# A chunked RWKV-7 block: the state's decay moves from TensorE and ScalarE to GpSimd and VectorE, and the output products get a stream of their own

## The chip, the cores and the metric

The kernel runs on one core of a Trainium2 chip, in one launch. A core has five engines that work at the same time, each through its own queue in order: PE (TensorE, matrix products into PSUM), ACT (ScalarE), DVE (VectorE), POOL (GpSimd, which also issues DMAs) and SP (which only issues DMAs). The metric is device time in microseconds (us) of one execution. Three runs of the kernel before gave 1114.17 to 1115.25, median 1114.42 us.

## The reference

It is one block of a network for a sequence of 512 tokens of width 1024: an RWKV-7 time mix with 16 heads of width 64, a depthwise convolution of 31 taps beside it, a gated merge of the two, and a feed-forward of width 2816. What matters here is the recurrence of the time mix. Each head has a 64 x 64 state that decays and takes a rank-one update at every token:

```python
def step(S, inp):
    r_t, w_t, k_t, v_t, a_t, b_t = inp
    sa = jnp.einsum('bhvk,bhk->bhv', S, a_t)
    S = S * w_t[:, :, None, :] + sa[..., None] * b_t[:, :, None, :] + v_t[..., None] * k_t[:, :, None, :]
    y = jnp.einsum('bhvk,bhk->bhv', S, r_t)
    return S, y
```

Its `y` is normalized per head, gets a bonus and a gate, and is multiplied by `w_rwkv_out`; the convolution's result is normalized over all channels and multiplied by `w_conv_out`.

## The kernel before

All arrays lie with channels on the 128 partitions and the 512 tokens along the free axis, so there are 8 channel tiles (`ct` 0 to 7), of two heads each. Large products are done in three matmuls on a value and its rounding rest (`acc3`: high by high, high by low, low by high); one such output tile is 24 matmuls of 128x512, called `dn` in the profile. Weights come in halves of 256 KB: on POOL's queue by two DMAs (`wh`, and `wl`, which adds the weights onto a copy that ACT has negated) or, when `sc.fast` is off, on SP's queue by one DMA (`wf`) and a subtraction on DVE.

The recurrence is done in 8 chunks of 64 tokens per channel tile. For each channel tile `prep` builds the decayed keys, `solve` inverts the triangular systems of all chunks, `values` lays out the values, and `chain(ct)` goes through the 8 chunks one after the other. One step of the chain is: a product of the state `SV` with the keys (`zt<-SV,AR`), a copy by ACT (`zs`), a product with the inverse (`zt<-zs,Pbd`), two copies by ACT (`UV`), and the update of the state. For the update PE adds the old state itself, as a product with the identity matrix (`zt<-SV,cs` in the profile, since the identity lies in the tile `cs`), and the product `zt<-UV,bkT` on top of it in PSUM; two ACT instructions of 64x64, one for each head, multiply the sum by the decay of the chunk `dL` and write the next `SV`. The first chunk has no old state, the last makes no next one, so there are 6 identity products in a chain and 48 in all, and 7 pairs of ACT instructions in a chain. The output products `yp` are issued in the chain itself, in two halves, after the fourth chunk and after the last.

The order of the instructions around this is set by a planner (`Sched`). Each stream records its instructions; the planner has a cost for every kind of instruction, keeps a clock for each engine, and takes from the heads of all streams the one that can start first, within 0.15 us the one of the most urgent priority: chain 0, `prep` and `values` 2, `solve` and `finish` 3, large products 4, the 31 taps of the convolution (`taps`, on DVE) 5. What comes out is a fixed order on each engine; on the chip an engine waits at the head of its queue, whatever stands behind. Streams wait for events, which are posted when all that was recorded ahead of them has been issued: `chain(ct)` waits for `("chain", ct - 1)`, `("val", ct)` and `("solve", ct)`; `solve(ct)` waits for `("chain", ct - 1)` before it writes the inverse tile `Pbd`, of which there is one.

The taps are 31 passes of DVE over a 128x512 tile for each channel tile (`cacc` and `cpad` are their two running sums, `ca` holds their input and their result). When all 8 are done, `conv_norm` normalizes and writes `CH` and `CL`, which the products of `w_conv_out` read. Behind the chains come the products of the gates and of `w_rwkv_out`, then those of `w_conv_out`, `w_out` and the feed-forward, all of them `dn` matmuls.

Of the kernel before, what the change touches and what calls it, by code (L numbers as in the profile page):

```python
# [9 lines left out]
F32 = mybir.dt.float32  # L10
F32R = mybir.dt.float32r
I32 = mybir.dt.int32
AF = mybir.ActivationFunctionType
ALU = mybir.AluOpType
# [3 lines left out]
P = 128  # L18
# [4 lines left out]
L = 64  # L23
NCH = T // L
# [6 lines left out]
WK = 4  # L31
WB = 6
WT = 4
LB = {"mu_r": 2, "mu_k": 2, "mu_v": 1}
NWO = 3
BUFS = (2, 2, 2, 2, 2, 1, 1)
# [45 lines left out]
def tile_hybrid_block(ctx, tc, xT, cst, prm, dwp, wl1, w2g, w_in, w_ro, w_co, w_o,  # L82
# [277 lines left out]
    sc = Sched()  # L360
# [18 lines left out]
    V, G, S = Engine("DVE", nc.vector), Engine("POOL", nc.gpsimd), Engine("ACT", nc.scalar)  # L379
    PE, SY = Engine("PE", nc.tensor), Engine("SP", nc.sync)  # L380

    def pool(stack, name, bufs, **k):
        return Pool(stack.enter_context(tc.tile_pool(name=name, bufs=bufs, **k)), bufs)

    cp = pool(ctx, "cp", 1)
    wp = pool(ctx, "wp", WT)
    turn = itertools.count()
    tp = pool(ctx, "tp", 1)
    sp = pool(ctx, "sp", 2)
# [3 lines left out]
    py = pool(ctx, "py", 1, space=PSUM)  # L393

    def tmp(name, tag=None, bufs=1, cols=T):
        return tp.tile([P, cols], F32, tag=tag or name, bufs=bufs, name=name)
# [9 lines left out]
    ident = cs[:, C_ID:C_ID + P]  # L406
# [10 lines left out]
    def vec(name, ct, lo=0, hi=P):  # L417
        j = VECS.index(name) * NT + ct
        return pr[lo:hi, j:j + 1]
# [7 lines left out]
    def der(d, ct):  # L427
        return drv[:, d * NT + ct:d * NT + ct + 1]

    E, O = slice(0, 64), slice(64, 128)  # L430
# [40 lines left out]
    def colstat(dst, src, rhs, blocks=4):  # L471
        for b in range(blocks):
            PE.matmul(dst(b), lhsT=src[:, b * P:(b + 1) * P], rhs=rhs, start=True, stop=True)

    def bcast(ps, lhs, blocks=4):
        for b in range(blocks):
            PE.transpose(ps[:, b * P:(b + 1) * P], lhs(b), ident)

    def spread(r8, rx):
        S.activation(out=rx.rearrange("p (a v) -> p a v", v=HD),  # L480
                     in_=r8.unsqueeze(2).to_broadcast([P, 8, HD]), func=AF.Copy)


    def rsqrt(v, n):
        y, t, w = (sp.tile([P, n], F32, tag=g_, bufs=2, name=g_) for g_ in ("ry", "rt", "rw"))
        V.tensor_scalar(out=y.bitcast(I32), in0=v.bitcast(I32), scalar1=-0.5, scalar2=RSQ,
                        op0=ALU.mult, op1=ALU.add)
        for _ in range(3):
            V.tensor_mul(t, v, y)
            V.scalar_tensor_tensor(out=w, in0=t, scalar=-0.5, in1=y, op0=ALU.mult, op1=ALU.mult)  # L490
            V.scalar_tensor_tensor(out=y, in0=w, scalar=1.5, in1=y, op0=ALU.add, op1=ALU.mult)
        return y
# [72 lines left out]
    for k in range(NT):  # L565
        if k == WK:
# [4 lines left out]
                               op0=ALU.mult, op1=ALU.subtract)  # L571
# [11 lines left out]
    def normed():  # L583
        for k in range(NT):
# [7 lines left out]
                    op0=ALU.mult, op1=ALU.add)  # L592
# [3 lines left out]
                    op0=ALU.mult, op1=ALU.add)  # L596
# [7 lines left out]
    def act(n_):  # L604
        if n_ not in acts:
            acts[n_] = hp.tile([P, NT, T], F32, tag=n_, name=n_)
        return acts[n_]
# [73 lines left out]
    def ktmp(name, bufs=1, cols=T):  # L681
        pool = kp if name in ("mu_v", "ep") else kq
        return pool.tile([P, cols], F32, tag=name, bufs=bufs, name=name)

    def lerp(ps, dmu, nm, ct):
        t_ = ktmp(nm, bufs=LB[nm])
        S.activation(out=t_, in_=ps, func=AF.Identity, scale=der(dmu, ct))
        V.scalar_tensor_tensor(out=t_[:, 1:T], in0=ps[:, 0:T - 1], scalar=vec(nm, ct),
                               in1=t_[:, 1:T], op0=ALU.mult, op1=ALU.add)
        return t_  # L690
# [41 lines left out]
    def low_out(ct, c0, n, nm):  # L732
        wf_, wh_, wl_ = (wp.tile([P, n], d_, tag=nm + x_, bufs=1, name=nm + x_)
                         for x_, d_ in (("f", F32), ("h", F32R), ("l", F32R)))
        SY.dma_start(out=wf_, in_=w2g[ct][:, c0:c0 + n])
        split(wf_, wh_, wl_)
        return wh_, wl_

    def lerp_of(key, dmu, nm, ct):
        def then(ps):  # L740
            st[ct][key] = lerp(ps, dmu, nm, ct)
        return then

    def once(fn):
        fn()
        yield from ()
# [209 lines left out]
    def chain(ct):  # L956
        s_ = st[ct]
        if ct:
            yield ("chain", ct - 1)
        yield ("val", ct)  # L960
        yield ("solve", ct)
        AR, GR, UV, SV, pb, bkT, dL = (s_[n] for n in ("AR", "GR", "UV", "SV", "pb", "bkT", "dL"))
        yp = None

        def outputs(cs_):
            for c in cs_:
                if c > 0:
                    for par, R in ((0, E), (1, O)):
                        PE.matmul(yp[R, c, :], lhsT=SV[R, c, par, :], rhs=AR[R, c, 2, :],
                                  start=c == 1, stop=False, skip_group_check=True)  # L970
            for c in cs_:
                for par, R in ((0, E), (1, O)):
                    PE.matmul(yp[R, c, :], lhsT=UV[:, c, par, :], rhs=GR[:, c, par, :],
                              start=False, stop=True, skip_group_check=True)

        for c in range(NCH):
            zt = pc.tile([P, 7, L], F32, tag="ch", name="zt")
            PE.matmul(zt[:, 0:2, :], lhsT=AR[:, c, 0:2, :], rhs=SV[:, c, :, :],
                      start=True, stop=True)
            zs = sp.tile([P, 2, L], F32, tag="zs", name="zs")  # L980
            S.activation(out=zs, in_=zt[:, 0:2, :], func=AF.Copy)
            PE.matmul(zt[:, 5:7, :], lhsT=pb[:, c, :], rhs=zs, start=True, stop=True)
            for par, R in ((0, E), (1, O)):
                S.activation(out=UV[R, c, par, :], in_=zt[R, 5 + par, :], func=AF.Copy)
            if c < NCH - 1:

                if c > 0:
                    PE.matmul(zt[:, 3:5, :], lhsT=ident, rhs=SV[:, c, :, :],
                              start=True, stop=False)
                PE.matmul(zt[:, 3:5, :], lhsT=bkT[:, c, :], rhs=UV[:, c, :, :],  # L990
                          start=c == 0, stop=True)
                for par, R in ((0, E), (1, O)):
                    S.activation(out=SV[R, c + 1, par, :], in_=zt[R, 3 + par, :], func=AF.Identity,
                                 scale=dL[R, c:c + 1])
            if c == NCH // 2 - 1:
                yp = s_["yp"] = py.tile([P, NCH, L], F32, tag="y", name="yp")
                outputs(range(0, NCH // 2))
        outputs(range(NCH // 2, NCH))
        sc.post(("chain", ct))
        sc.spawn(once(lambda: finish(ct)), 3)  # L1000

    def finish(ct):
        s_ = st[ct]
        g2 = low_out(ct, 2 * P, P, "g2")
        yp = s_["yp"].rearrange("p c t -> p (c t)")
        sq = tmp("sqy", "sq", 2)
        S.activation(out=sq, in_=yp, func=AF.Square)
        ys = tmp("ys")
        S.activation(out=ys, in_=yp, func=AF.Identity, scale=vec("gn_w", ct))
        ss = pm.tile([P, 4, WS], F32, tag="fi", bufs=1, name="ssy")  # L1010
        colstat(lambda b: ss[:, b, :], sq, sel2v)
        n0 = sp.tile([P, 8], F32, tag="n1", bufs=1, name="n1")
        V.tensor_scalar_add(n0.rearrange("p (a b) -> p a b", b=2), ss[:, :, 0:2], GN_EPS)
        r = rsqrt(n0, 8)
        rx = tmp("rxy", "sq", 2)
        spread(r, rx)
        bc = pm.tile([P, T], F32, tag="fi", bufs=1, name="bcy")
        bcast(bc, lambda b: rx[:, b * P:(b + 1) * P])
        V.tensor_mul(ys, ys, bc)
        V.scalar_tensor_tensor(out=ys, in0=ys, scalar=vec("gn_b", ct), in1=act("ya")[:, ct, :],  # L1020
                               op0=ALU.add, op1=ALU.add)
        gp = pm.tile([P, T], F32, tag="fi", bufs=1, name="gp")
        acc3(gp, *g2, [0], lambda k: GH, lambda k: GL, True, True)
        V.tensor_mul(act("ya")[:, ct, :], ys, gp)
        s_.clear()
        sc.post(("ya", ct))


# [94 lines left out]
    for ct in range(1, NT):  # L1123
        dense_tile(w_in[NT + ct], lerp_of("tk", D_OMK, "mu_k", ct), need=(("keys", ct - LB["mu_k"]),) if ct >= LB["mu_k"] else (),
                   ev=("k", ct))
# [5 lines left out]
    for ct in range(NT):  # L1131
        for g_, pri in ((prep, 2), (values, 2), (chain, 0), (taps, 5)):
            sc.spawn(g_(ct), pri)
# [19 lines left out]
    mid = {}  # L1153
# [222 lines left out]
    for h in range(2):  # L1376
        c = HALF[h]
# [83 lines left out]
```

## Time and profile before

| | |
|---|---|
| median of 3 runs | 1114.42 us |
| the profiled execution's own time | 1110.63 us |
| its span, first to last instruction | 1108.9 us |
| granted TensorE clock, mean | 0.986 |
| busy: PE, DVE, ACT, POOL | 1061.3, 731.5, 568.2, 103.8 us |

The profile is one execution. Its busy times are unions of the instructions' records; matmuls are pipelined, so their records overlap and a busy PE is not a PE at its peak. A row of a timeline has the start in us from the span's start, the time, the engine, the line, the operation, output<-inputs, the shape and the count; in brackets stands how long the engine had been idle and what ended it. Everything that the planner orders bears the number of the one line that issues it, so groups are told apart by the names of their tiles.

### The profile page before, as it was taken

Reading aid. Unit: us, or ns where it says so; the run is one execution under the profiler, and the core shown is the slowest. Engines: PE = TensorE matmul, PEld = TensorE weight load, DVE = VectorE, ACT = ScalarE, POOL = GpSimd, SP = SyncE. Lnnn points to the kernel's source line nnn. Section 1 sums busy time; section 2 is a strip of 40 time slices with the busy share of each in tenths; the row PEclk is TensorE's granted clock in tenths of the full one; section 3 lists DMA queues with packets and bytes.
Section 4 is the critical chain, followed back from the end, with each engine's and each line's share of the span. In section 5 each row is a group of like instructions: output and inputs, shape, how many; then the busy total and the mean of one; then the engine's idle time right before and its main releaser. Section 6 shows DMA issues by size and latency. Waiting matters only on the chain.

```text
span 1108.9 us, 18596 instructions
## 1 busy us (share of the span) xinstructions
PE 1061.3 (96%) x7066; PEld 860.2 (78%) x7066; DVE 731.5 (66%) x1511; ACT 568.2 (51%) x1197; POOL 103.8 (9%) x172
## 2 busy tenths in 40 slices
PE   7799999999899999989999999999999999999996
PEld 5577787877787777768788888998888888888885
DVE  5878899899898999998553366365444444433324
ACT  5556666777777777555572235344333333323321
POOL 0003322211313222010000000000000000000000
PEclk9899999999899999999999999999999999999998
DMA  6115745434546454144232236102223222333312
GB/s 240 46 40 119 145 98 122 82 70 95 104 98 122 102 114 101 33 86 152 77 105 96 87 104 204 62 1 81 93 94 95 95 95 95 91 100 115 105 48 76
DMA packets 68872, 107.74 MB, mean 97 GB/s; under 512 B 15152, under 2 KB 20656, under 8 KB 68784
## 3 DMA queue, kind: packets, MB, share of 16 engines
q1 hardware_dynamic: 48912, 70.38, 20.2%
q0 software_dynamic: 19872, 36.18, 16.2%
q8 instruction: 56, 0.92, 0.3%
q14 instruction: 32, 0.26, 0.1%
HBM read 102.34 MB, written 2.10 MB: 94 GB/s over the span
## 4 chain that ended last, share of the span: by engine, by line
PE 83%; DVE 6%; ACT 4%; issue 1%; DMA 0%; DVEq 0%; ACTq 0%
PE dn L225 34%; PE dn L300 29%; PE zt L300 5%; PE psf L225 2%; PE wo L225 2%; PE yp L300 2%; PE gps L300 1%; ACT Mt L300 1%; PE lora L300 1%; DVE AR L300 1%; DVE GR L300 1%; DVE cacc L300 1%; DVE cpad L300 1%; PE ssy L300 1%; PE psn L225 1%
## 5 line engine op out<-in xcount | busy, mean ns | idle before, releaser
L225 ACT ACTIVATE wh<-wf 128x512 fp32r<-128x512 f32 x140 | 86.7, 619 | 219.2 <-PE dn L225 209.3
L225 DVE TENSOR_TENSOR wl<-wf,wh 128x512 fp32r<-128x512 f32 x140 | 94.4, 675 | 125.2 <-ACT wh L225 125.0
L300 PE MATMUL dn<-HH,wh 128*128 128x512 f32 x408 | 168.8, 414 | 0.0
L300 PE MATMUL dn<-HH,wl 128*128 128x512 f32 x408 | 168.1, 412 | 0.0
L300 PE MATMUL dn<-HL,wh 128*128 128x512 f32 x408 | 167.4, 410 | 0.0
L225 PE MATMUL dn<-FHL,wh 128*128 128x512 f32 x320 | 127.7, 399 | 0.0
L225 PE MATMUL dn<-FHH,wh 128*128 128x512 f32 x320 | 126.2, 394 | 0.0
L225 PE MATMUL dn<-FHH,wl 128*128 128x512 f32 x320 | 125.4, 392 | 0.0
L225 PE MATMUL dn<-FH,wh 128*128 128x512 f32 (+1 forms) x332 | 101.3, 388 | 0.0
L300 PEld LDWEIGHTS dn<-HH,wl 128*128 128x128 f32 x408 | 78.0, 191 | 14.4 <-issue 0.5
L300 PEld LDWEIGHTS dn<-HH,wh 128*128 128x128 f32 x408 | 77.8, 191 | 14.6 <-issue 0.7
L300 PEld LDWEIGHTS dn<-HL,wh 128*128 128x128 f32 x408 | 77.7, 190 | 14.6 <-issue 0.5
L300 ACT ACTIVATE wh<-wf 128x512 fp32r<-128x512 f32 x69 | 42.9, 627 | 78.5 <-PE dn L300 71.2
L300 DVE SCALAR_TENSOR_TENSOR cacc<-ca,dw,cacc 128x512 f32<-128x512 f32 x105 | 78.1, 744 | 0.0
L300 POOL DMA_DIRECT2D wl<-in_w_in_dram x69 | 60.4, 886 | 180.8 <-ACT wl L300 149.0
L300 DVE SCALAR_TENSOR_TENSOR cpad<-ca,dw,cpad 128x512 f32<-128x512 f32 x98 | 73.0, 745 | 0.1
L300 DVE TENSOR_TENSOR wl<-wf,wh 128x512 fp32r<-128x512 f32 x69 | 47.3, 688 | 38.6 <-ACT wh L300 38.6
L225 PEld LDWEIGHTS dn<-FH,wh 128*128 128x128 f32 x332 | 61.5, 188 | 13.9
L225 PEld LDWEIGHTS dn<-FHH,wh 128*128 128x128 f32 x320 | 60.1, 188 | 15.7
L225 PEld LDWEIGHTS dn<-FHH,wl 128*128 128x128 f32 x320 | 60.1, 188 | 14.3
L225 PEld LDWEIGHTS dn<-FHL,wh 128*128 128x128 f32 x320 | 60.1, 188 | 13.6
L225 PE MATMUL dn<-FH,wl 128*128 128x512 f32 (+1 forms) x166 | 64.0, 385 | 0.0
(306 smaller groups left out, 2101.6 us busy)
## 6 DMA issues: line engine op xcount, KB each, us to landing
wh<-in_w_in_dram POOLq DMA_DIRECT2D x69, 256.0 KB, 3.8
wl<-in_w_in_dram POOLq DMA_DIRECT2D x69, 256.0 KB, 4.4
wf<-in_w_gt_dram SPq DMA_DIRECT2D x44, 256.0 KB, 2.6
wf<-in_w_up_dram SPq DMA_DIRECT2D x44, 256.0 KB, 2.6
wf<-in_w_in_dram SPq DMA_DIRECT2D x43, 256.0 KB, 2.8
wf<-in_w_dn_dram SPq DMA_DIRECT2D x40, 256.0 KB, 2.7
wf<-in_w_ro_dram SPq DMA_DIRECT2D x16, 256.0 KB, 2.5
wf<-in_w_co_dram SPq DMA_DIRECT2D x16, 256.0 KB, 2.6
```

Of the source, the lines that this page charges most:

```text
L225: return fn(*a, **k)
L300: i = fn(*a, **k)
```

## The change

The identity product is left out: `zt<-UV,bkT` alone stands in PSUM. From the second chunk of a chain to the last but one, two POOL instructions of 64x64 multiply the old state by the decay into a new tile `dS` (two buffers), and two DVE instructions multiply the product by the same decay and add `dS`, which gives the next `SV`. The first chunk's state is still written by ACT. The output products are recorded by a stream of their own (`out_stream`, priority 1): its first half waits for `("mid", ct)`, posted after the fourth chunk, and for `("fin", ct - 1)`, posted when `finish` of the tile before has read `yp`; its second half for `("state", ct)`, posted at the chain's end. `("chain", ct)` is now posted by this stream, and `chain(ct)` waits for `("state", ct - 1)` in its place.

```diff
+OP = 1
...
         if ct:
-            yield ("chain", ct - 1)
+            yield ("state", ct - 1)
...
+        def out_stream():
+            yield ("mid", ct)
+            if ct:
+                yield ("fin", ct - 1)
+            outputs(range(0, NCH // 2))
+            yield ("state", ct)
+            outputs(range(NCH // 2, NCH))
+            sc.post(("chain", ct))
+            sc.spawn(once(lambda: finish(ct)), 3)
+
+        sc.spawn(out_stream(), OP)
         for c in range(NCH):
...
                 if c > 0:
-                    PE.matmul(zt[:, 3:5, :], lhsT=ident, rhs=SV[:, c, :, :],
-                              start=True, stop=False)
+                    dS = sp.tile([P, L], F32, tag="dS", name="dS")
+                    for par, R in ((0, E), (1, O)):
+                        G.tensor_scalar(out=dS[R], in0=SV[R, c, par, :], scalar1=dL[R, c:c + 1],
+                                        scalar2=None, op0=ALU.mult)
                 PE.matmul(zt[:, 3:5, :], lhsT=bkT[:, c, :], rhs=UV[:, c, :, :],
-                          start=c == 0, stop=True)
+                          start=True, stop=True)
                 for par, R in ((0, E), (1, O)):
-                    S.activation(out=SV[R, c + 1, par, :], in_=zt[R, 3 + par, :], func=AF.Identity,
-                                 scale=dL[R, c:c + 1])
+                    if c > 0:
+                        V.scalar_tensor_tensor(out=SV[R, c + 1, par, :], in0=zt[R, 3 + par, :],
+                                               scalar=dL[R, c:c + 1], in1=dS[R], op0=ALU.mult,
+                                               op1=ALU.add)
+                    else:
+                        S.activation(out=SV[R, c + 1, par, :], in_=zt[R, 3 + par, :],
+                                     func=AF.Identity, scale=dL[R, c:c + 1])
             if c == NCH // 2 - 1:
...
+                sc.post(("mid", ct))
+        sc.post(("state", ct))
```

The planner makes a new order of this. On PE, at the middle of chain 0, before (`yp` are the output products, `bck`, `ss` and `wps` those of `prep` and `solve`, `dn` the large ones):

```order
L300 MATMUL zt<-SV,cs 128x128
L300 MATMUL zt<-UV,bkT 128x128
L300 MATMUL yp<-AR,SV 64x64 x6
L300 MATMUL yp<-GR,UV 64x64 x8
L300 MATMUL bck<-cs,kkn 128x128
```

and of the change, the same place on PE:

```order
L301 MATMUL zt<-UV,bkT 128x128
L301 MATMUL dn<-HH,wh 128x512
L301 MATMUL dn<-HL,wh 128x512
L301 MATMUL bck<-cs,kkn 128x128
L301 MATMUL yp<-AR,SV 64x64 x6
L301 MATMUL zt<-SV,AR 128x128
L301 MATMUL yp<-GR,UV 64x64 x8
L301 MATMUL zt<-zs,Pbd 128x128
```

The identity product is gone, and the two groups of `yp` now stand around the next step's first product in place of ahead of it. At the end of chain 0 they stand right ahead of `xps`, the product that the next inverse waits for, in both orders.

On POOL, at the first steps of chain 0, where before only the DMAs `wh` and `wl` of the weights stood, the change has a library instruction (`ISA`) and the decays `dS` between the DMAs:

```order
L301 DMA wl<-in_w_in_dram 128x512
L301 ISA
L301 TENSOR_SCALAR dS<-SV,dL 64x64 x2
L301 DMA wl<-in_w_in_dram 128x512
L301 DMA wh<-in_w_in_dram 128x512
L301 TENSOR_SCALAR dS<-SV,dL 64x64 x2
L301 DMA wl<-in_w_in_dram 128x512
L301 TENSOR_SCALAR dS<-SV,dL 64x64 x2
```

The `ISA` stands once in the program, ahead of the first decay; it makes POOL load the library that the decays need. POOL goes from 69 to 78 pairs of weight DMAs, SP from 43 to 34 of `wf` from `w_in`, and DVE from 201 to 192 subtractions of 128x512. Of the 48 pairs of decays 19 stand right behind a `wl` DMA.

On DVE, in chain 0, the updates of the state stand among the taps and the work of `prep`, where before there was nothing of the chain:

```order
L301 SCALAR_TENSOR_TENSOR SV<-zt,dL,dS 64x64 x2
L301 TENSOR_SCALAR cpad_94<-ca,dw 128x512
L301 SCALAR_TENSOR_TENSOR cacc<-ca,dw,cacc 128x512
L301 SCALAR_TENSOR_TENSOR cpad_94<-ca,dw,cpad_94 128x512
L301 SCALAR_TENSOR_TENSOR cacc<-ca,dw,cacc 128x512
L301 SCALAR_TENSOR_TENSOR cpad_94<-ca,dw,cpad_94 128x512
L301 SCALAR_TENSOR_TENSOR SV<-zt,dL,dS 64x64 x2
```

A step of the chain has some five passes of DVE between two updates. Taps move back: behind the first DVE instruction of the last `finish` there stood 4 taps before, and now 37.

## Rows read from the trace of the kernel before

**Rows 1.** The page: busy times, and the span in 40 slices, in tenths
```profile
PE 1061.3 (96%) x7066; PEld 860.2 (78%) x7066; DVE 731.5 (66%) x1511; ACT 568.2 (51%) x1197; POOL 103.8 (9%) x172
...
PE   7799999999899999989999999999999999999996
...
DVE  5878899899898999998553366365444444433324
```

**Rows 2.** Stretches of the 8 chains: start:end, length, then busy us (and instructions)
```profile
core 0: us, PE busy (x) PEld busy (x) DVE busy (x) ACT busy (x) POOL busy (x), PEclk, DMA share, GB/s
141.80:173.00 31.20, 31.20 (x395) 25.71 (x394) 29.58 (x78) 22.00 (x60) 9.39 (x13) 1.00 0.53 110
...
469.40:500.00 30.60, 26.13 (x174) 20.25 (x175) 27.84 (x51) 18.91 (x54) 5.22 (x6) 0.94 0.40 78
sum 251.60, PE 241.80 PEld 195.86 DVE 233.88 ACT 175.89 POOL 53.89; mean PE 30.23 PEld 24.48 DVE 29.24 ACT 21.99 POOL 6.74
```

**Rows 3.** What PE waited for from 141.8 to 500: us, times, longest
```profile
PE zt L300 <- ACT SV L300: 3.7, 5, 0.9
```

**Rows 4.** Timeline of PE in a step of chain 0
```profile
160.44 0.38 PE L300 MATMUL zt<-SV,cs 128*128 128x128 f32 x2
160.66 0.39 PE L300 MATMUL zt<-UV,bkT 128*128 128x128 f32 x2
```

**Rows 5.** Instructions that touch the tile zt: ns min/median/max, first and last start
```profile
L300 PE MATMUL zt<-SV,cs x96: 270/274/418, 147.7 to 495.2; 128*128 128x128 f32 x96
...
L300 ACT ACTIVATE SV<-zt,dL x112: 291/309/312, 144.8 to 496.1; 64x64 f32<-64x64 f32 x112
```

**Rows 6.** Groups of DVE instructions by shape: busy us, mean ns | idle before
```profile
L300 DVE SCALAR_TENSOR_TENSOR cacc<-ca,dw,cacc 128x512 f32<-128x512 f32 x105 | 78.1, 744 | 0.0
...
L300 DVE SCALAR_TENSOR_TENSOR rw<-rt,ry 128x8 f32<-128x8 f32 x48 | 8.0, 166 | 1.5
...
L300 DVE TENSOR_TENSOR P<-P,xqs 128x128 f32<-128x128 f32 x8 | 2.3, 282 | 0.1
```

**Rows 7.** Instructions that touch the tile CH: ns min/median/max, first and last start
```profile
L300 PE MATMUL dn<-CH,wh x64: 399/399/399, 628.5 to 672.6; 128*128 128x512 f32 x64
...
L300 DVE TENSOR_TENSOR CL<-ca,CH x8: 684/692/694, 550.9 to 577.4; 128x512 fp32r<-128x512 f32 x8
```

**Rows 8.** Groups of POOL instructions by shape: busy us, mean ns | idle before
```profile
L300 POOL DMA_DIRECT2D wl<-in_w_in_dram x69 | 60.4, 886 | 180.8 <-ACT wl L300 149.0 <-PE zt L300 13.3 <-ACT zs L300 13.1
L300 POOL DMA_DIRECT2D wh<-in_w_in_dram x69 | 41.8, 610 | 110.0 <-PE dn L300 100.1 <-PE zt L300 8.8 <-issue 0.8
L300 POOL MEMSET SV<- 64x64 f32 x16 | 3.8, 240 | 0.5
```

**Rows 9.** The tile SV: its clearing on POOL
```profile
L300 POOL MEMSET SV<- x16: 144/146/527, 67.7 to 430.1; 64x64 f32 x16
```

**Rows 10.** Timeline at the second step of chain 0, POOL, ACT and PE
```profile
145.06 0.88 POOL L300 DMA_DIRECT2D wl<-in_w_in_dram  x1 [0.20 <-issue]
...
148.54 0.62 ACT L300 ACTIVATE SV<-zt,dL 64x64 f32<-64x64 f32 x2
...
147.91 0.39 PE L300 MATMUL zt<-UV,bkT 128*128 128x128 f32 x2
```

**Rows 11.** A table load of ACT, from its groups; a DMA of POOL, us to landing
```profile
L300 ACT ACT_TABLE_LOAD x9 | 11.5, 1283 | 0.2
...
wl<-in_w_in_dram POOLq DMA_DIRECT2D x69, 256.0 KB, 4.4
```

**Rows 12.** Timeline of ACT, two state updates in a row
```profile
157.11 0.63 ACT L300 ACTIVATE SV<-zt,dL 64x64 f32<-64x64 f32 x2
...
161.26 0.31 ACT L300 ACTIVATE SV<-zt,dL 64x64 f32<-64x64 f32 x1
```

**Rows 13.** What POOL waited for: us, times, longest
```profile
POOL wl L300 <- ACT wl L300: 149.0, 34, 26.4
```

More of the change, by code (lines that the diff above doesn't have):

```diff
@@ L962, in chain @@
         AR, GR, UV, SV, pb, bkT, dL = (s_[n] for n in ("AR", "GR", "UV", "SV", "pb", "bkT", "dL"))
-        yp = None
         def outputs(cs_):
+            if cs_[0] == 0:
+                s_["yp"] = py.tile([P, NCH, L], F32, tag="y", name="yp")
+            yp = s_["yp"]
             for c in cs_:
@@ L987, in chain @@
                 if c > 0:
-                    PE.matmul(zt[:, 3:5, :], lhsT=ident, rhs=SV[:, c, :, :],
-                              start=True, stop=False)
+                    dS = sp.tile([P, L], F32, tag="dS", name="dS")
+                    for par, R in ((0, E), (1, O)):
+                        G.tensor_scalar(out=dS[R], in0=SV[R, c, par, :], scalar1=dL[R, c:c + 1],
+                                        scalar2=None, op0=ALU.mult)
                 PE.matmul(zt[:, 3:5, :], lhsT=bkT[:, c, :], rhs=UV[:, c, :, :],
-                          start=c == 0, stop=True)
+                          start=True, stop=True)
                 for par, R in ((0, E), (1, O)):
-                    S.activation(out=SV[R, c + 1, par, :], in_=zt[R, 3 + par, :], func=AF.Identity,
-                                 scale=dL[R, c:c + 1])
-            if c == NCH // 2 - 1:
[L996 to L1000, printed above, removed]
+                    if c > 0:
[5 more added lines that the diff above has]
+                                     func=AF.Identity, scale=dL[R, c:c + 1])
+            if c == NCH // 2 - 1:
+                sc.post(("mid", ct))
+        sc.post(("state", ct))
     def finish(ct):
@@ L1009, in finish @@
         S.activation(out=ys, in_=yp, func=AF.Identity, scale=vec("gn_w", ct))
+        sc.post(("fin", ct))
         ss = pm.tile([P, 4, WS], F32, tag="fi", bufs=1, name="ssy")
@@ L1024, in finish @@
         V.tensor_mul(act("ya")[:, ct, :], ys, gp)
-        s_.clear()
         sc.post(("ya", ct))
```

## The prediction

> **What bounds the kernel now.** I read the page first: the reader is to see that PE is busy in nearly every slice to the end, while DVE is at eight or nine tenths only up to slice 19 and falls behind it [rows 1]. So the end is set by PE behind about 500 us, and DVE is nearly as full as PE only in the stretch of the chains. Then I cut that stretch into its 8 chains, each from its first product to its last: of 251.6 us PE is busy 241.8, DVE 233.88, ACT 175.89, POOL 53.89 [rows 2]. DVE has 251.6 - 233.9 = 17.7 us free in all eight, 2.2 us in a chain. The list of waits shows that PE rarely stands for the state: 5 times, 3.7 us together, behind ACT's `SV` [rows 3]. Large products fill the chain's latency. Hence a chain does not end sooner because a step's latency shrinks; it ends sooner if PE has less to do, and later if an engine that the steps go through becomes fuller than PE. Of the taps only the end matters: the last `CL` starts at 577.4 us and the products that read `CH` and `CL` start at 628.5 [rows 7], so DVE's deferrable work has 628.5 - 578.1 = 50 us of room, 578.1 being 577.4 and one pass of 0.69.
>
> **PE: the identity products.** In the timeline the identity product starts at 160.44 and the next one at 160.66 [rows 4], so it takes 0.22 us of PE's time, though its records (two passes each, 96 in all) are 0.274 us long and overlap [rows 5]. 48 x 0.22 = 10.6 us less on PE, all of it in the chains' stretch. It is a gain only where PE is what fills the stretch.
>
> **ACT and DVE: who writes the state.** ACT loses 96 of 112 instructions of 0.309 us [rows 5], 29.7 us; ACT has 75 us free in the chains [rows 2], so by itself this is worth nothing. DVE gets 96 instructions of 64x64 with one operand in PSUM. The trace has none: an 8-column one takes 0.166 us, a 128-column one from PSUM 0.282 [rows 6], and between them at 64 columns 0.166 + 0.116 x 56/120 = 0.22. That is 96 x 0.22 = 21 us on an engine with 17.7 us free. The order answers it: 33 more taps stand behind the last chain, 33 x 0.744 = 24.6 us [rows 6], and they end up in the 50 us of room, at no cost. So the planner's own sum is even. If that cover were gone (a conv that ends over 50 us later), the products of `w_conv_out` would wait.
>
> What is new is that DVE's queue now holds a link of the chain. Behind a waiting update stand taps, the lerps that free PE's accumulators and the work of `prep`; PE waits for the next state, and behind its first product stand all large products.
>
> **POOL: the decays, and what they do to DVE.** Two decays of 64x64 must be done between one state and the next update. The time for it is 161.26 - 157.74 = 3.5 us, from the end of one update (157.11 + 0.63) to the start of the next [rows 12]. The trace shows POOL only clearing such tiles, 0.144 us at the least, 0.240 mean [rows 8, 9]. A decay also reads what it writes, so I take twice the least clearing, 0.3 us; its bounds are 0.144 and the 0.886 of a `wl` DMA [rows 8]. Two of them, 0.6 us, fit into 3.5. The open price is what DVE loses while POOL reads. The lower bound is nothing: the 16 clearings ran beside a DVE that was 93% busy in the chains, and their median of 0.146 us is all but their minimum [rows 2, 9]; but they read nothing. The upper bound is a whole tap for each decay, 0.744 us [rows 6], 71 us in all. I take DVE to stand for the length of the decay, 0.3 us, which lies nearer to the clearing than to the tap: 96 x 0.3 = 28.8 us. DVE's free 17.7 us take the first part, 28.8 - 17.7 = 11.1 us remain and lengthen the chains, since the order on DVE is fixed and an update stands behind some five passes. PE's stretch, 10.6 us lighter, is then not what fills it, and that gain is lost in waits.
>
> The Trainium skill speaks on this: "SBUF — State Buffer", section "Who interferes with whom", has a VectorE instruction with two SBUF inputs and a GpSimd instruction that reads SBUF exclude each other for a whole instruction, and not one that only writes. The taps have two such inputs. No run here shows a reading POOL instruction; the clearings only write, and their median agrees. By this rule a decay that comes first holds a tap back for its 0.3 us, which is what the sum has; without it the loss would be nothing, and the time that of the first rival below.
>
> **POOL: the library.** The `ISA` stands in the queue behind the `wl` DMA that ends at 145.06 + 0.88 = 145.94, ahead of the first decay [rows 10]. No row has its price. The nearest are ACT's table load, 1.283 us, and a DMA of POOL to its landing, 4.4 us [rows 11]; as the code has to be fetched, I take 4.4. Then the first `dS` is there at 145.94 + 4.4 + 0.6 = 150.9. It is needed at 148.5, when ACT starts that update now [rows 10]: 2.4 us of standing for PE, behind whose next product of the chain all large products stand. With 1.283 us the decay would be there at 147.8 and the cost nothing.
>
> By the Trainium skill, "GPSIMD Engine Reference", section "Instruction dispatch", the first call of a freshly loaded kernel pays about 6 us, with no instruction visible. The standing would be 4.0 us in place of 2.4 and the time 1.6 us more; an estimate from that page, and no run here shows it yet.
>
> **The DMAs and the stream of outputs.** Nine halves of weights go from SP to POOL, which gets 9 x (0.886 + 0.610) = 13.5 us [rows 8] and is 21% busy in the chains [rows 2]; DVE loses nine passes of its late work. Both are hidden. The output products are the same in number; at the middle of a chain they move by one product, and at its end they stand right ahead of `xps` as before, so the next inverse and the next chain are released by the same instructions. I cost this at nothing; a wait for `finish` of the tile before is covered by a chain's 30 us.
>
> **The sum.** 2.4 for the library, 11.1 for DVE, and nothing for PE's 10.6: 13.5 us, from the profiled execution's 1110.63 (span 1108.9) to 1124.1. The runs' median lies 3.8 us above that execution; on its scale 1127.9, so 1128 us.
>
> **Rivals.** *Decays that cost DVE nothing.* If POOL reads beside the taps as freely as it clears, DVE's sum is even and PE fills the chains: -10.6, with 0 to 2.4 for the library, -8.2 to -10.6 and 1104 to 1106. For it speaks that PE is 96% busy and hardly waits [rows 1, 3]; against it, that DVE has 17.7 us free and each decay of more than 17.7/96 = 0.18 us of DVE's time turns the sign. That 0.18 is the point from which it decides. Chance 0.3.
>
> *POOL's queue.* 19 of the 48 pairs stand behind a `wl` DMA, which waits for ACT's copy, 4.4 us in the mean (149.0/34) [rows 13]. If all of that wait fell behind the state, the decays would be there 4.4 + 0.9 + 0.6 = 5.9 us after it, 2.4 too late: 19 x 2.4 = 45.6, less 10.6, plus 2.4, some 37 us more, 1152. It decides from 2.0 us of wait behind the state (3.5 - 0.9 - 0.6). Against it: these waits are idle time, most of which lies ahead of the state. Chance 0.12.
>
> *Even.* DVE loses about 0.2 us for each decay, or the gain pays just for the library: within 2 us of before. Chance 0.08.
>
> **The numbers.** The forecast has 0.5, with a range of its own from 1114 to 1147 (0.18 to 0.5 us of DVE's time for a decay: -0.4 and +30.3, and the library's 0 to 2.4). The whole range takes in the first rival and most of the second: 1104 to 1150, with some 2 in 10 outside. What a measurement here can tell from no change is 0.2%, 2.2 us. Faster by more 0.30, within 0.10, slower 0.60.
>
> **What would show it.** In the trace after: 96 decays on POOL of about 0.3 us; taps next to a decay longer than 0.744 or with idle time ahead of them; the step of the chain, now 161.26 - 157.11 = 4.15 us [rows 12], longer by about half a us in the middle of a chain; PE's waits for DVE's `SV` several us in all, where ACT's are 3.7 now; and a gap on POOL ahead of the first decay. The forecast is wrong if the taps keep 0.744 us back to back and the chains' stretch is shorter by some 10 us; or if POOL's decays start late behind `wl` DMAs.

## The result, and the profile after

The changed kernel takes 1125.02 us (median of 4 runs, 1124.05 to 1125.37), the kernel before beside it 1114.30 (1112.42 to 1115.25): a ratio of 1.0101, 95% interval 1.0080 to 1.0121. The profiled executions are 1125.37 and 1110.63 us long, with spans of 1123.6 and 1108.9. Forecast were 1128 us in all and 1124.1 on the scale of the profiled executions. The size came out, by luck: the terms it was added up from mostly did not, as shown below.

First the page of the changed kernel, the busy times and three lines of its 40 slices, against [rows 1].

```profile
PE 1063.2 (95%) x6970; PEld 851.0 (76%) x6970; DVE 756.3 (67%) x1598; ACT 537.7 (48%) x1101; POOL 167.6 (15%) x286
...
PE   7799999999899999879999999999999999999996
...
DVE  4878898889799989989965356384444444433324
...
PEclk9899999999899999969999999999999999999998
```

The clock's line of the kernel before:

```profile
PEclk9899999999899999999999999999999999999998
```

PE has 96 instructions fewer and is busy 1.9 us longer. Two things are new: from 449 to 506 us PE's slices have an 8 and a 7 where they had a 9 and an 8, and the clock has a 6 in the second of them where it had a 9. The same stretches in numbers come from the windows, first of the kernel before, then of the changed one: up to the chains' first product, from there to the last chain's last `AR` product, to the first product that reads `MH`, and to the end (columns: start:end, length, then busy us of each engine, the granted clock, the DMA's share, GB/s).

```profile
0.00:141.80 141.80, 123.25 (x742) 95.86 (x743) 109.60 (x213) 81.71 (x147) 22.29 (x43) 0.96 0.44 116
141.80:496.50 354.70, 337.30 (x3447) 269.14 (x3445) 324.72 (x787) 252.91 (x656) 81.55 (x129) 0.98 0.46 95
496.50:673.30 176.80, 175.87 (x802) 142.26 (x802) 99.93 (x166) 81.63 (x132) 0.00 (x0) 1.00 0.33 106
673.30:1108.90 435.60, 424.85 (x2079) 352.93 (x2077) 197.28 (x348) 151.99 (x262) 0.00 (x0) 0.99 0.28 89
```

```profile
0.00:143.00 143.00, 124.12 (x743) 96.38 (x744) 109.60 (x213) 81.86 (x147) 22.25 (x43) 0.96 0.44 115
143.00:512.30 369.30, 338.21 (x3351) 259.86 (x3349) 330.32 (x844) 221.94 (x559) 135.74 (x230) 0.96 0.45 91
512.30:688.40 176.10, 175.81 (x801) 141.90 (x802) 117.97 (x194) 81.75 (x133) 9.59 (x14) 1.00 0.42 120
688.40:1123.60 435.20, 425.07 (x2079) 352.84 (x2077) 198.44 (x350) 152.19 (x262) 0.00 (x0) 0.99 0.29 89
```

The lead-in grew by 1.2 us, the last two stretches shrank by 1.1 together; the loss lies between the first and the last `AR` product, 369.3 - 354.7 = 14.6 us. Inside it, measured from a chain's first `AR` product to its last, the eight chains are as long as they were (223.8 after, 224.7 before); the seven gaps between them grew from 130.0 to 145.6. Behind it PE is full (0.3 us idle in 176), as it was.

VectorE is not what fills this stretch: it has 369.3 - 330.3 = 39.0 us free there, 30.0 before. PE comes nearest to full, and behind the chains it is full, so PE's time is closed as a sum. In this account the stretch runs from the chains' first product to the first that reads `MH`, which holds the same 1412 weight products in every kernel here (1401 in the reordered one below, where 11 more stand ahead). It is PE's work at full clock, plus PE's idle time, plus what the lower clock costs. For the last term two pairs of rows from the changed kernel's timeline of PE (columns: start, us, engine, line, operation, tiles, shape, count): weight products follow each other by 0.43 us at about 498 us, where the clock is 1.2 GHz, and by 0.23 us at 499.2, where it is 2.4.

```profile
497.67 0.63 PE L301 MATMUL dn<-HL,wh 128*128 128x512 f32 x1
498.10 0.63 PE L301 MATMUL dn<-HH,wl 128*128 128x512 f32 x1
...
499.17 0.40 PE L301 MATMUL dn<-HL,wh 128*128 128x512 f32 x1
499.40 0.39 PE L301 MATMUL dn<-HH,wl 128*128 128x512 f32 x1
```

Half of PE's busy time at 1.2 GHz is therefore counted as lost. All figures are us, from the profiled executions:

| kernel | stretch | PE work | PE idle | at 1.2 GHz | lost by clock |
|---|---|---|---|---|---|
| before | 531.5 | 506.4 | 18.3 | 13.7 | 6.8 |
| changed | 545.4 | 500.5 | 31.4 | 30.7 | 13.5 |
| difference | +13.9 | -5.9 | +13.1 | +17.0 | +6.7 |

The sum closes by its definition; what it tells is which term grew. The work column is good to some 5 us only: the kernel before with the early gate, below, has the same instructions and 501.9.

The profiled pair is no exception in the clock. Every execution has its mean granted clock on record, and the span times what is missing to 1 is an estimate of what the clock takes, if PE is taken as always busy: 24.7 us in the mean of the changed kernel's executions, 17.3 to 18.3 in the groups of the kernel before.

Where PE stood is in its waits from 141 to 520 us (us in total, times, longest), against [rows 3].

```profile
PE zt L301 <- DVE SV L301: 10.6, 29, 0.9
...
PE xps L301 <- DVE ya L301: 1.7, 1, 1.7
PE ssy L301 <- ACT sqy L301: 1.7, 1, 1.7
```

It waits 29 times for the state that VectorE writes, where 5 waits for ACT's had 3.7 us. The two single waits lie in the last gap. There PE has no weight products left in either kernel; its timeline in the changed kernel shows it standing twice, and the clock falls to 1.2 GHz right behind, at 481.8.

```profile
475.55 1.12 PE L301 MATMUL bps<-mu_r,cs 128*128 128x512 f32 x2
478.40 0.69 PE L301 MATMUL xps<-P,Wt 32*32 32x32 f32 x32 [1.73 <-DVE ya L301]
480.78 1.07 PE L301 MATMUL ssy<-cs,sqy 128*128 128x16 f32 x8 [1.68 <-ACT sqy L301]
481.69 0.65 PE L301 MATMUL zt<-SV,AR 128*128 128x128 f32 x2
```

The same place in the kernel before:

```profile
466.42 1.13 PE L300 MATMUL bps<-mu_r,cs 128*128 128x512 f32 x2
467.41 1.07 PE L300 MATMUL ssy<-cs,sqy 128*128 128x16 f32 x8
468.40 0.69 PE L300 MATMUL xps<-P,Wt 32*32 32x32 f32 x32
```

`ssy`, the norm of the tile before, stood ahead of `xps` and covered the wait for `ya`; now that `finish` is released from the outputs' stream it stands behind `xps` and ahead of the next chain.

Last the instructions that the forecast had priced: the update and the decay by the tiles they touch (ns min/median/max), a tap from the groups of VectorE, and GpSimd's timeline at its first decays.

```profile
L301 DVE SCALAR_TENSOR_TENSOR SV<-zt,dL,dS x96: 234/284/292, 149.6 to 511.9; 64x64 f32<-64x64 f32 x96
L301 POOL TENSOR_SCALAR dS<-SV,dL x96: 432/443/1352, 147.3 to 508.4; 64x64 f32<-64x64 f32 x96
```

```profile
L301 DVE SCALAR_TENSOR_TENSOR cacc<-ca,dw,cacc 128x512 f32<-128x512 f32 x105 | 78.4, 747 | 0.2
```

```profile
146.24 0.88 POOL L301 DMA_DIRECT2D wl<-in_w_in_dram  x1 [0.21 <-issue]
147.26 0.97 POOL L301 TENSOR_SCALAR dS<-SV,dL 64x64 f32<-64x64 f32 x2
```

An update takes 0.284 us at the median (forecast 0.22), a decay 0.443 (forecast 0.3). A tap has a mean of 747 ns against 744 [rows 6], hardly moved. The first pair of decays begins 147.26 - 147.12 = 0.14 us behind the DMA ahead of it and takes 0.97: nothing of the library's loading is seen.

The longest decay took 1.352 us, and the trace shows why. Of the 96 decays 19 took more than 0.6 us, and 18 of these began while a VectorE pass over 512 columns with two inputs in SBUF was under way. One of them, the second decay of its pair, between two taps:

```profile
372.61 0.75 DVE L301 SCALAR_TENSOR_TENSOR cacc<-ca,dw,cacc 128x512 f32<-128x512 f32 x1
372.89 0.79 POOL L301 TENSOR_SCALAR dS<-SV,dL 64x64 f32<-64x64 f32 x1
373.28 0.81 DVE L301 SCALAR_TENSOR_TENSOR cpad<-ca,dw,cpad 128x512 f32<-128x512 f32 x1
```

It ends 0.31 us behind the pass that it met, as 14 of the 18 do, so it stood until that pass was nearly over; two others stood through a second pass too. The tap behind it takes 0.81 us in place of 0.744. Decays that began beside no pass of over 0.48 us (64 of them) took 0.432 to 0.493, and the 7 that began beside a pass with one of its inputs in PSUM 0.441 to 0.447. So where a decay meets a tap, it is mostly GpSimd that stands: 7.9 us over all 96, counted above 0.443 each. VectorE in turn stands for no decay: the list of its waits from 141 to 545 us has none.

### The profile page after: what moved, and what is told of

Its sections match the earlier page's. It is cut to its first block, busy times and chain, and to the rows that moved or that the text cites. A ratio compares the mean times of both kernels' runs of the same rounds, so it can differ in the third digit from the quotient of the medians.

```text
span 1123.6 us, 18592 instructions
## 1 busy us (share of the span) xinstructions
PE 1063.2 (95%) x6970; PEld 851.0 (76%) x6970; DVE 756.3 (67%) x1598; ACT 537.7 (48%) x1101; POOL 167.6 (15%) x286
## 3 DMA queue, kind: packets, MB, share of 16 engines
q0 software_dynamic: 22464, 40.90, 18.3%
## 4 chain that ended last, share of the span: by engine, by line
PE 68%; DVE 19%; issue 3%; ACT 2%; DMA 2%; DVEq 0%; ACTq 0%
PE dn L226 33%; PE dn L301 21%; DVE SV L301 2%; DVE cacc L301 2%; PE psf L226 2%; PE zt L301 2%; DVE Ps L301 2%; DVE cpad L301 2%; DVE tt L301 2%; PE wo L226 2%; PE gps L301 1%; PE lora L301 1%; DMA SV<-UV 1%; ACT Mt L301 1%; DVE AR L301 1%
## 5 line engine op out<-in xcount | busy, mean ns | idle before, releaser
L226 ACT ACTIVATE wh<-wf 128x512 fp32r<-128x512 f32 x140 | 86.6, 619 | 219.0 <-PE dn L226 206.4
L226 DVE TENSOR_TENSOR wl<-wf,wh 128x512 fp32r<-128x512 f32 x140 | 94.1, 673 | 122.6 <-ACT wh L226 122.5
L301 PEld LDWEIGHTS dn<-HH,wl 128*128 128x128 f32 x408 | 78.2, 192 | 13.6 <-issue 0.5
L301 POOL DMA_DIRECT2D wl<-in_w_in_dram x78 | 69.4, 902 | 108.9 <-ACT wl L301 82.8
L226 PEld LDWEIGHTS dn<-FH,wh 128*128 128x128 f32 x332 | 61.5, 188 | 13.9
L226 PEld LDWEIGHTS dn<-FHH,wl 128*128 128x128 f32 x320 | 60.1, 188 | 15.5
L226 PEld LDWEIGHTS dn<-FHH,wh 128*128 128x128 f32 x320 | 60.1, 188 | 13.7
L301 ACT ACTIVATE wh<-wf 128x512 fp32r<-128x512 f32 x60 | 37.1, 626 | 62.3 <-PE dn L301 54.3
L301 POOL TENSOR_SCALAR dS<-SV,dL 64x64 f32<-64x64 f32 x96 | 50.1, 522 | 87.5 <-DVE SV L301 67.7
```

What stands on the lines that cost most here:

```text
L226: return fn(*a, **k)
L301: i = fn(*a, **k)
```

## The experiments

Letters stand for theories. A: GpSimd's decays slow VectorE (the forecast). B: VectorE's load stretches the gaps. C: the stream of outputs releases the next chain later. D: PE is the bound, and its waits and its clock are the loss. E: any other order of the instructions would lose as much. The kernel before, timed again beside each group of these kernels, has medians from 1112.5 to 1113.9 us. Each ratio is to the kernel before of its own group; differences of medians from two groups carry about 1 us of this drift.

**The outputs' stream alone.** The changed kernel with the old update:

```
-  G.tensor_scalar(out=dS[R], in0=SV[R, c, par, :], ...)
+  PE.matmul(zt[:, 3:5, :], lhsT=ident, rhs=SV[:, c, :, :], start=True, stop=False)
-  V.scalar_tensor_tensor(out=SV[R, c + 1, par, :], ...)
+  S.activation(out=SV[R, c + 1, par, :], in_=zt[R, 3 + par, :], func=AF.Identity, scale=dL[...])
```

> Only the second part of the change: the output products in their own stream, the state update as before (identity product on PE, two ACT scalings). Theory A, the forecast's (GpSimd's decays slow VectorE's taps, the stream costs nothing): as before, 1113 to 1116 us. Theory B (the 27 us of state updates put on VectorE, 96 of 0.284 us, stretch the gaps between the chains, where it is already 90% busy): also as before, 1112 to 1117. Theory C (the stream posts the chain's end later, so that the next inverse's last product and with it the next chain begin later; 26 weight products, 6 us, stand in the way in the gap after the second chain): most of the loss is here, 1120 to 1126.

Measured: 1124.26 us, ratio 1.0098 (1.0062 to 1.0134). The part that the forecast costed at nothing loses by itself about as much as both, inside C's range. Its profiled execution (1119.61, the shortest of the four) has 30.7 us at 1.2 GHz in the stretch, like the changed kernel, and 22.7 us idle.

**The state update alone.** The kernel before with the decays and the additions, `outputs` called inside the chain:

> Only the first part: the state update on GpSimd and VectorE, the output products inside the chain as before. Theory A: all of the loss, 1123 to 1127. Theory B: all of the loss too, 1122 to 1127, with the growth in the gaps between the chains. Theory C: 1110 to 1116, a little faster if the identity products that went (48 of 0.22 us, 10.6 us) are worth anything.

Measured: 1125.52 us, 1.0104 (1.0064 to 1.0144). This alone costs all of it too, so the loss is neither A nor B nor C alone: the two share something. In its profiled execution (1118.81, the shortest of the four) PE's work is 9 us less than before (497.4), its idle time 30.2, and again 30.7 us run at 1.2 GHz.

**The inverse released by the state.** In `solve` of the changed kernel:

```
-            yield ("chain", ct - 1)
+            yield ("state", ct - 1)
```

> The changed kernel, but the next chain's inverse waits for the end of the state chain and no longer for the last output products, which don't read what it overwrites. Theories A and B: 1124 to 1126, nothing is won. Theory C: the 6 us in the gap after the second chain and some in the others come back, 1114 to 1120.

Measured: 1124.85 us, 1.0103 (1.0069 to 1.0136). Nothing is won: the gap after the second chain falls from 25.4 to 23.7 us, but the one after the fourth grows to 30.2, and 44.4 us run at 1.2 GHz. A late release of the inverse is not the loss.

**VectorE scales, GpSimd rests.** The changed kernel with the identity product back on PE, and the state scaled out of PSUM by VectorE:

```
+  PE.matmul(zt[:, 3:5, :], lhsT=ident, rhs=SV[:, c, :, :], start=True, stop=False)
+  V.tensor_scalar(out=SV[R, c + 1, par, :], in0=zt[R, 3 + par, :], scalar1=dL[R, c:c + 1], ...)
```

> The changed kernel with the identity product kept on PE and the state scaled out of PSUM by VectorE (96 instructions, as many as in the changed kernel) in place of ACT; GpSimd decays nothing. Theory A: without reads by GpSimd the 11 us go, 1112 to 1116. Theory B: VectorE carries as much as in the changed kernel, 1122 to 1127. Theory C: as the changed kernel, 1123 to 1127, since the stream is as in it; its gaps tell it from B only together with the run that has the stream alone.

Measured: 1138.28 us, 1.0235 (1.0206 to 1.0263), above every expectation. There is no decay on GpSimd, and PE's waits are these:

```profile
PE zt L301 <- DVE SV L301: 14.5, 31, 1.9
```

So the waits come from VectorE as the writer of the state, without any read by GpSimd. Against the changed kernel PE's work is 9.6 us more (510.1), idle time 30.6, the clock's loss 4.9 more: the 48 identity products, 10.6 us in the forecast, show nearly in full in PE's work. A falls as the cause of these waits.

**The planner's prices.** The changed kernel; only the order moves:

```
+ t = 0.45 if name == "tensor_scalar" else 0.2 + 1.2e-3 * n      # POOL
...
+ if name == "scalar_tensor_tensor" and n == L and psum:         # DVE
+     return 0.31, 0.45, 0.0
```

> The changed kernel, with the planner's prices for the two new operations set to what the trace of the changed kernel shows (an update on VectorE 0.31 us, its result 0.45 us after its start in place of 0.226, a decay on GpSimd 0.45 us in place of 0.277); only the order of the instructions changes. Theory D (PE is the bound from the first chain to the output projections; in the changed kernel its products there cost 10 us less, but it stands 14 us longer, 7 of them in front of the chain's AR products, which the planner put too early, and it runs 17 us longer at 1.2 GHz): the waits of PE for the state on VectorE fall from 10.6 to about 4 us, and the time to 1114 to 1119. Theory B (VectorE's load is the bound): 1123 to 1127, since VectorE has the same work. Theory E (the numbers that set the order suit the order of the kernel before, and any other order loses about 10 us): 1120 to 1128, whatever the waits do.

Measured: 1126.66 us, 1.0137 (1.0096 to 1.0177). D was half right: the waits went as it said, the time did not.

```profile
PE zt L304 <- DVE SV L304: 3.8, 5, 1.3
```

Idle time fell from 31.4 to 24.2 us, but the time at 1.2 GHz doubled to 61.4 us, 26.9 us lost. The order now uses up the weight products earlier (23 stand in the seventh chain, 49 before), and 30.7 us of the slow clock begin at 463.

**Products for the last gap.** The changed kernel with one condition less:

```
     dense_tile(w_in[6 * NT + m], lambda ps, m=m: gate_c(m, ps),
-               need=(("inner", NT - 1), ("val", NT - 1)))
+               need=(("inner", NT - 1),))
```

> The changed kernel, in which the eight gate projections may start when the last chain's inputs are prepared, without waiting for its values; so PE has 17 weight products instead of none between the last two chains, where it stood 3.8 us and ran 17.1 us at 1.2 GHz right after. Theory D with the clock as part of the loss: the stretch at 1.2 GHz near 482 us shrinks to some 3 us, and the kernel is 6 to 10 us faster, 1115 to 1119. Theory B: no more than 2 us, 1123 to 1126, since VectorE has no less to do. Theory E: 1120 to 1128.

Measured: 1108.50 us, 0.9965 (0.9950 to 0.9979): 16.5 us less than the changed kernel in the medians (15 by the two ratios), more than D expected, and faster than the kernel before. The windows of the last gap and the last chain show it, in the changed kernel, then with the gate early (columns as above):

```profile
473.00:481.60 8.60, 4.75 (x78) 3.38 (x78) 6.78 (x11) 5.38 (x16) 0.42 (x1) 1.00 0.68 170
481.60:512.30 30.70, 26.13 (x123) 19.02 (x122) 26.89 (x57) 13.04 (x35) 16.73 (x23) 0.72 0.43 72
```

```profile
473.00:480.60 7.60, 7.43 (x88) 5.63 (x88) 7.57 (x12) 6.01 (x15) 2.00 (x3) 1.00 0.55 112
480.60:507.60 27.00, 25.56 (x154) 19.49 (x153) 25.96 (x56) 12.62 (x36) 14.55 (x23) 1.00 0.55 111
```

PE was busy 4.75 of 8.60 us in the gap, and the chain behind it ran at 0.72 of the clock; filled to 7.43 of 7.60, the chain runs at 1.00, is 3.7 us shorter and holds 31 more of PE's instructions. The waits for the state are still there, so the two losses are separate:

```profile
PE zt L301 <- DVE SV L301: 9.4, 27, 1.0
```

B falls too: VectorE has the same work, and the seven gaps are still 144.3 us long, so their growth was not by itself the loss.

**The kernel before, reordered.** One meaningless number of the planner moved:

```
- LAG = {"PE": 0.15, "ACT": 0.15, ...}
+ LAG = {"PE": 0.15, "ACT": 0.16, ...}
```

> The kernel before, with one number of the planner moved that means nothing on the chip (the lag it counts after an instruction of ACT 0.16 in place of 0.15 us): the same instructions in another order. Theory D and theory B: 1111 to 1118, about as before, since all work stays where it was. Theory E: 1120 to 1128, as far from before as the change itself.

Measured: 1113.19 us, 1.0006 (0.9990 to 1.0022). E falls as a general law, by one reordering; that some orders lose by the clock is still so.

**The kernel before with the early gate.** The same line as above:

> The kernel before with the gate projections let in as early as in the other run (8 weight products instead of none between the last two chains). Theory D: PE's 4.5 us of standing in the last chain and the 3.4 us at 1.2 GHz there shrink, 1107 to 1112. Theory B: 1112 to 1116. Theory E: 1112 to 1116 too, since the order up to the last chain stays as it is.

Measured: 1101.98 us, 0.9905 (0.9881 to 0.9928). That is more than any theory expected. The starved gap was a loss of the kernel before too, 11 us; in the changed one it is 15 to 16.5. Their difference, some 5 us, is what the change loses there, and 1108.5 - 1102.0 = 6.5 us is what it loses elsewhere. The last gap and the last chain of the kernel before:

```profile
463.70:469.40 5.70, 4.79 (x79) 3.54 (x79) 5.63 (x12) 5.27 (x14) 0.00 (x0) 1.00 0.28 60
469.40:496.50 27.10, 22.63 (x132) 17.29 (x132) 25.17 (x47) 17.39 (x49) 5.22 (x6) 0.94 0.43 80
```

By the estimate from the granted clock of every execution, the clock takes 15.5 us of the changed kernel with the early gate and 16.5 of the kernel before with it; without the gate it took 6 to 7 us more of the changed kernel than of the kernel before. So what the change lost in the starved gap was, by this estimate, mostly the clock.

**The two parts, each with the early gate.** First the update alone:

> The state update of the change alone, output products in the chain as before, gate projections let in early. Theory D: PE waits for the updates on VectorE as in the changed kernel, so like it, 1105 to 1109; the identity products that went show in PE's work, not in the time. Theory E: anywhere from 1100 to 1112.

Then the outputs' stream alone:

> The output products' stream alone, state update as before, gate projections let in early. Theory D: no waits for VectorE's updates and no starved gap before the last chain, so like the kernel before with the early gate, 1101 to 1105. Theory C (the stream releases the next chain later and that costs): 1106 to 1112.

Measured: 1107.85 us, 0.9956 (0.9939 to 0.9974), and 1104.92, 0.9927 (0.9911 to 0.9942). With the last gap filled the parts come apart: 5.9 us for the update, 2.9 for the stream (its interval and that of the kernel before with the early gate overlap), 6.5 for both. PE's waits for the state, first with the update alone, then with the stream alone:

```profile
PE zt L300 <- DVE SV L300: 9.8, 23, 1.6
```

```profile
PE zt L301 <- ACT SV L301: 1.9, 3, 1.0
```

**Twice the decays.** The changed kernel with the early gate; 96 more decays into a tile that nobody reads, all else in the same order:

```
+  for par, R in ((0, E), (1, O)):
+      G.tensor_scalar(out=dX[R], in0=SV[R, c, par, :], scalar1=dL[R, c:c + 1], ...)
```

> The changed kernel with the gate projections let in early (1108.5 us), and every decay on GpSimd followed by a second, unused one of the same operands and size (96 more, about 0.45 us each); the planner counts them as nothing, so all else stands in the same order. Theory A, the forecast's (each decay costs VectorE 0.3 us by slowing its operations): 15 to 29 us more, 1123 to 1138, and the taps lengthen. Theory D (PE's idle time and its clock are the loss, and GpSimd's reading costs VectorE nothing): 1107 to 1112, taps of 0.745 us as they are.

Measured: 1115.71 us, 1.0020 (1.0006 to 1.0035), 7.2 us more: outside both expectations. The groups of VectorE and GpSimd:

```profile
L303 DVE SCALAR_TENSOR_TENSOR cacc<-ca,dw,cacc 128x512 f32<-128x512 f32 x105 | 78.9, 752 | 0.2
```

```profile
L303 POOL TENSOR_SCALAR dX<-SV,dL 64x64 f32<-64x64 f32 x96 | 53.5, 558 | 7.9
```

A tap is 752 ns, with the early gate alone 746:

```profile
L301 DVE SCALAR_TENSOR_TENSOR cacc<-ca,dw,cacc 128x512 f32<-128x512 f32 x105 | 78.4, 746 | 0.2
```

As the order is the same, each instruction of VectorE can be set beside its own: from 140 to 546 us all of them together are 2.8 us longer, 0.03 us for each added decay. PE's idle time in the account is 28.3 us in place of 22.3. So reading by GpSimd costs VectorE a tenth of the forecast. The decays bear the rest of what the two engines do to each other: 53 of the 192 took more than 0.6 us, 19 of 96 with the early gate alone. How the 53 us more in GpSimd's queue make the time 7.2 us longer is not shown; only 2 updates waited for a decay, 0.5 us together.

**Both repairs.** Early gate and measured prices:

> The changed kernel with both: the gate projections let in early, and the measured prices for the updates and decays in the planner. Theory D: PE stands no longer in front of the chain's AR products (some 7 us less idle than with the gate alone, which had 22.0 in the stretch from the first to the last of them), and with products at hand in the last two chains the clock doesn't fall as it did with the prices alone (61 us at 1.2 GHz): 1099 to 1104, no slower than the kernel before with the early gate (1102.0). Theory E (orders differ by luck): anywhere from 1103 to 1115.

Measured: 1110.23 us, 0.9981 (0.9965 to 0.9996). A miss for D, inside E's range. The waits fell as expected, from 9.4 to 3.0 us, and idle time to 17.9:

```profile
PE zt L304 <- DVE SV L304: 3.0, 3, 1.4
```

PE's work is the least of all (492.7 us), yet 44.4 us ran at 1.2 GHz, 21.3 us lost. Two windows of this kernel in which the clock fell:

```profile
268.00:290.00 22.00, 18.25 (x253) 13.90 (x252) 19.52 (x52) 11.72 (x29) 7.50 (x14) 0.69 0.27 56
460.00:482.00 22.00, 19.59 (x245) 15.83 (x244) 16.00 (x37) 8.78 (x25) 10.00 (x17) 0.69 0.56 100
```

PE was busy 18.25 and 19.59 of 22 us there, at 0.69 of the clock. The second is the seventh chain, which has 49 weight products in this order and 60 with the early gate alone. Whether that is what brings the clock down stays open. The fastest of all is the kernel before with the early gate, 1101.98 us.

## Why the prediction was right, and where its steps were not

The sign and the size were right: 10.7 us in the medians, 13.6 forecast. The sum behind it was not, and that it came out so near is luck: neither of its two terms, 11.1 us for VectorE and 2.4 for the library, was there, and about as much came from waits for the state, a starved gap and the clock, for which it had no term.

*What bounds.* The forecast let VectorE take PE's place as what fills the chains' stretch. It did not: VectorE has more time free there than before (39.0 against 30.0 us), and with the gate early the kernel is 16.5 us faster although VectorE has the same work. "That gain is lost in waits" is half right. PE's work fell, by 5.9 us in the account and by 2.4 to 9.0 in the pairs of kernels here that differ in the update alone (and in the order that follows from it), and its idle time rose by 13.1. But it stands for the state's longer way and in a gap without products, not behind a full VectorE.

*VectorE standing 0.3 us for each decay, 11.1 us.* This term failed. Doubling the decays lengthened VectorE's instructions by 0.03 us for each, 2.8 us in all; the time rose by 7.2, so added decays are not free, but not by this mechanism. The Trainium skill, "SBUF — State Buffer", section "Who interferes with whom", has a two-input VectorE instruction and a reading GpSimd instruction exclude each other for a whole instruction. The trace agrees that they get in each other's way, and shows who pays: 18 decays that met such a pass took 0.63 to 1.35 us in place of 0.443, while the tap right behind one loses 0.07 us, not a decay's length. The forecast reckoned only with a decay that comes first and holds the tap back, and left out the tap that comes first and holds the decay back. No update waited for a decay, so GpSimd's 7.9 us of standing do not show as waits of the chain.

*The rivals.* At 0.03 us for each decay the condition of the first one held (under 0.18), but its time, 1104 to 1106 us, did not come: it too had no term for the state's way or the gap. That of GpSimd's queue fails by the same list of VectorE's waits.

*The library, 2.4 us.* Zero: 0.14 us between the DMA and the first decay. The 6 us of the Trainium skill ("GPSIMD Engine Reference", "Instruction dispatch") are not seen in this execution either; whether an earlier one had loaded the code, the trace does not show.

*The update, 0.22 us, evened out by taps moved behind the chains.* It takes 0.284. The room behind the chains did cover the moved taps: the last `CL` begins at 617.6 us and the products that read it at 643.6. But the sum had no term for what the forecast itself named, a link of the chain in VectorE's queue. In the mean over the chains' 56 steps (48 of them with VectorE's update) the update begins 0.34 us after its product's modelled end, where ACT's began 0.14 after; from that end to the next `AR` product it is 1.11 us against 0.97. That is 56 x 0.14 = 7.8 us, near the growth of the waits (10.6 against 3.7 us). The planner's price, 0.226 us, put the `AR` product too early: with the measured price the waits fell to 3.8 and 3.0 us.

*The outputs' stream, nothing.* It cost about 10 us alone, and 2.9 with the last gap filled, which is hardly clear of noise. "Released by the same instructions" was true; but `ssy` changed places with `xps`.

*The clock.* No term had it: 6.7 us in the account, with 17.1 us of 1.2 GHz at 482 us where 3.4 were before, and 6 to 7 us by the granted clock of all executions. With the early gate that stretch is gone, the clock's loss falls from 13.5 to 8.5 us, and PE's idle time from 31.4 to 22.3.

So the measured loss, 11 us, is about 5 in the starved last gap with its clock and 6.5 elsewhere. The 6.5 are the waits for VectorE's update, perhaps a share of GpSimd's and the stream's, less what PE saves; how they split is not settled, because every run that took the waits away moved the clock as well.

## What to carry to other kernels

Close the bounding engine's time as a sum (work, idle, clock) before and after; a change that lightens it can still lose by where it then stands. An operation that is moved to another engine inside a latency chain costs the queue it joins, not only its duration, and a planner that does not know it places the consumer too early. When two halves of a change each cost as much as the whole, look for a weak place that they share: here one gap without work to fill it, worth more than the change. And where two engines may shut each other out, ask which of them stands, and whether anything waits for it.

## What the runs showed of the hardware

A GpSimd instruction of 64x64 that reads SBUF (0.443 us) stood when it met a VectorE pass of 512 columns with two SBUF inputs: 18 such decays took 0.63 to 1.35 us, most of them ending 0.31 us behind the pass. Beside passes with one input in PSUM 7 decays took 0.441 to 0.447 us. The taps lost little: 0.07 us where one began right behind a decay that had stood, 3 to 8 ns in the mean over all of them. VectorE's update from PSUM at 64 columns took 0.280 us in the mean, with a third operand from SBUF and as a plain scaling alike. And the clock can hide a change of this size: between the kernels here PE ran 13.7 to 61.4 us of one stretch at 1.2 GHz, which by the account cost 5.8 to 26.9 us.
